# Thresholded attention on one core: the stages of a pair of heads placed by a plan of 22 steps

## The chip, the cores and the metric

One core of a Trainium2 chip runs the kernel once per launch. The metric is device time in microseconds, the median of three runs. TensorE (PE) is granted one of two clocks, 1.2 GHz or 2.4 GHz; the profile shows it as a share, 0.50 or 1.00. The other engines of this kernel are ScalarE (ACT), VectorE (DVE), GpSimd (POOL), whose queue here issues transfers, and SyncE (SP), which only issues transfers.

## The reference

Attention in f32 for 8 x 12 heads of 512 rows and 64 columns, with a cut: weights at or below 0.1 become zero, and what is left is normalised again.

```python
batch, heads, seq, dim = 8, 12, 512, 64          # threshold 0.1
scores = np.einsum('bhqd,bhkd->bhqk', Q, K) * scale
weights = softmax(scores)
weights = np.where(weights > threshold, weights, 0)
weights = weights / (np.sum(weights, axis=-1, keepdims=True) + 1e-10)
return np.einsum('bhqk,bhkd->bhqd', weights, V)
```

A row in which no weight exceeds 0.1 has an output of zero. With these inputs that is most rows.

## The kernel before

The kernel works on pairs of heads, 48 of them. The output is first filled with zeros, 256 KB per pair, from a tile of zeros (`do_load`, L174). Then a cheap screen in bf16 finds the rows that may have a weight above the threshold, at most 64 per head; these alone are gathered, computed exactly in f32, and scattered over the zeros.

A pair takes these stages, each a function of the code:

- **load** (SP): Q and K of the pair in four transfers, and the fill with zeros. **vload** (POOL): V, as bf16.
- **Q and K transposes** `do_tr` (PE, L180): four 128x128 f32 transposes each, into one PSUM bank; evicted by ACT (`do_qev` L186, `do_kev` L192). DVE centres K (`do_kcentre`).
- **scores** `do_qk` (PE, L227): in each of four steps two matmuls of 128x512, one per head, on the two halves of the array; **screen** `do_screen`: per step two score tiles, reduced by ACT (exponential with a sum, L241) or by DVE (maximum, L244). Of the eight tiles of a pair ACT takes five and DVE three.
- **squares, norms, normev**: a check of the norms that the screen's margin relies on (DVE, PE, ACT).
- **flags** (DVE, L248), **rank** (PE, L256 and L258), **key** (DVE, keys and the one-hot oh), **idx** (PE, L277), **gather** (DVE idx, L283, then POOL's indirect DMA, L284): from the flags of 512 rows the list of the selected ones, and their rows of Q.
- **split** (DVE, qb, L294), **xtr** (PE, L301), **xev** (ACT, xq, L307): the gathered rows, transposed.
- **xqk** (PE, L312): their exact scores, f32, in two passes of the profile's rows; **xexp** (ACT, e, L318), **xmask** (DVE, tv L324 and the mask m L326).
- **xpt** (PE, L334): four bf16 transposes of m; **xptev** (DVE, pt, L340); **xpv** (PE, L349 and L352): output and row sums; **xout**: the reciprocal rcp (DVE, L359 and L360), the scaled result res (ACT, L362) and the scatter (POOL, L363).

One loop of steps g runs over 4 steps a pair, hp being the pair whose scores the step makes, qi = 0 to 3. Each step issues the scores and stages of several pairs: of the next pair (its transposes), of this one, and of those one to four back. Every compute instruction and POOL's transfers keep the order in which the program gives them, per engine (`keep`); each engine takes its own list in order, and waits on semaphores for the others. The scheduler places the loads, with five buffers each for Q and K. The order by hand, before:

- qi 0: flags and rank of hp-1, Q transpose of hp+1, xqk of hp-3, screen, xptev of hp-4, squares of hp.
- qi 1: K transpose of hp+1, xpv of hp-4, screen, key of hp-1, the K eviction, xexp of hp-3.
- qi 2: idx of hp-1, screen, gather of hp-1, kcentre of hp+1, xmask of hp-3, split of hp-2, xout of hp-4.
- qi 3: xtr of hp-2, xpt of hp-3, norms of hp, vload, screen, xev of hp-2, normev of hp.

PSUM has eight banks: five for 128x512 f32 tiles (`spsum`: scores, transposes, xqk), one for the transposed mask (`ptpsum`), two small ones (`mpsum`, tag sm: norms, rank, idx, xtr, xpv). A stage that takes a bank waits until the last reader of its previous tile is done.

The fill with zeros and the scatter write the same DRAM tensor. The scheduler orders them against each other: a scatter waits until the fill ahead of it in its order has landed, and the next fill waits until that scatter has landed. This holds before and after the change.

At the end the kernel checks that no head had more than 64 selected rows and no norm was too large; otherwise a loop at the end computes everything without the screen. With these inputs it isn't entered.

Of the kernel before, what the change touches and what calls it, by code (L numbers as in the profile page):

```python
# [11 lines left out]
def kernel(  # L12
# [122 lines left out]
    nc.gpsimd.memset(cuts[:, 1, 0:SO - 1], CUT * CS / scale)  # L135
# [12 lines left out]
    ptpsum = ctx.enter_context(tc.tile_pool(name="ptpsum", bufs=1, space=bass.MemoryType.PSUM))  # L148
    mpsum = ctx.enter_context(tc.tile_pool(name="mpsum", bufs=2, space=bass.MemoryType.PSUM))
# [8 lines left out]
    qb_t, sq_t, nm_t = {}, {}, {}  # L158
# [25 lines left out]
    def do_qev(hp, sc):  # L184
        qk = tpool.tile([P, 2, SO * P], SCREEN)
        keep(nc.scalar.copy(qk[:, 0, :], sc[:]))  # L186
        qk_t[hp] = qk

    def do_kev(hp, sc):
# [17 lines left out]
    def do_norms(hp):  # L207
        nm = mpsum.tile([P, P], f32, name="sm")
# [22 lines left out]
    def do_screen(g):  # L231
# [5 lines left out]
        for h2 in range(2):  # L237
            sc = sc_t.pop((g, h2))
            if h2 == 0 or qi == SO - 1:
# [12 lines left out]
    def do_rank(hp):  # L252
        f = f_t[hp]
        rk = mpsum.tile([P, P], f32, name="sm")
# [18 lines left out]
    def do_idx(hp):  # L273
        oh = oh_t.pop(hp)[:].rearrange("p h s r -> p r (h s)")
        ix = mpsum.tile([P, P], f32, name="sm")
# [23 lines left out]
    def do_xtr(hp):  # L299
        xp = mpsum.tile([P, P], f32, name="sm")  # L300
# [29 lines left out]
    def do_xpt(hp):  # L330
        m = m_t.pop(hp)
        pt = ptpsum.tile([P, SO, P], bf16)
# [10 lines left out]
    def do_xpv(hp):  # L343
        pt, v_bf = pts_t.pop(hp), v_in.pop(hp)
        o = mpsum.tile([P, P], f32, name="sm")
# [10 lines left out]
    def do_xout(hp):  # L356
        o = o_t.pop(hp)
        rcp = small.tile([P, 1], f32)
        keep(nc.vector.tensor_scalar_add(rcp[:], o[:, D:D + 1], 1e-10))  # L359
        keep(nc.vector.reciprocal(rcp[:], rcp[:]))  # L360
        res = outp.tile([P, D], f32)
        keep(nc.scalar.activation(res[:], o[:, 0:D], ACTF.Copy, scale=rcp[:, 0:1]))  # L362
        keep(nc.gpsimd.indirect_dma_start(  # L363
            out=Or, out_offset=bass.IndirectOffsetOnAxis(ap=ix_t.pop(hp)[:, 0:1], axis=0),
            in_=res[:], in_offset=None, element_offset=hp * 2 * S * D, bounds_check=2 * S - 1, oob_is_err=False))
# [6 lines left out]
    do_qev(0, do_tr(q_in.pop(0)))  # L372
    do_kev(0, do_tr(k_in.pop(0)))
# [4 lines left out]
    def has(hp):  # L378
        return 0 <= hp < NP

    for g in range((NP + 5) * SO):
# [6 lines left out]
        if qi == 0:  # L388
            if has(hp - 1):
                do_flags(hp - 1)  # L390
                do_rank(hp - 1)
            if has(nxt):
                tr = do_tr(q_in.pop(nxt))
            if has(hp - 3):
                do_xqk(hp - 3)
            if g < G:
                do_screen(g)
            if has(nxt):
                do_qev(nxt, tr)
            if has(hp - 4):  # L400
                do_xptev(hp - 4)
            if has(hp):
                do_squares(hp)
        elif qi == 1:
            if has(nxt):
                tr = do_tr(k_in.pop(nxt))
            if has(hp - 4):
                do_xpv(hp - 4)
            if g < G:
                do_screen(g)  # L410
            if has(hp - 1):
                do_key(hp - 1)
            if has(nxt):
                do_kev(nxt, tr)
            if has(hp - 3):
                do_xexp(hp - 3)
        elif qi == 2:
            if has(hp - 1):
                do_idx(hp - 1)
            if g < G:  # L420
                do_screen(g)
            if has(hp - 1):
                do_gather(hp - 1)
            if has(nxt):
                do_kcentre(nxt)
            if has(hp - 3):
                do_xmask(hp - 3)
            if has(hp - 2):
                do_split(hp - 2)
            if has(hp - 4):  # L430
                do_xout(hp - 4)
        else:
            if has(hp - 2):
                do_xtr(hp - 2)
            if has(hp - 3):
                do_xpt(hp - 3)
            if has(hp):
                do_norms(hp)
            if has(hp + 2):
                do_vload(hp + 2)  # L440
            if g < G:
                do_screen(g)
            if has(hp - 2):
                do_xev(hp - 2)
            if has(hp):
                do_normev(hp)
# [10 lines left out]
    over_t = mpsum.tile([P, P], f32, name="sm")  # L457
# [9 lines left out]
    with tc.If(many > 0):  # L467
        with tc.For_i(0, NP, 1) as hp:
# [9 lines left out]
            for qi in range(SO):  # L478
                for h2 in range(2):
# [12 lines left out]
                    pt_ps = ptpsum.tile([P, SO, P], bf16, name="pt")  # L492
# [5 lines left out]
                    o = mpsum.tile([P, P], f32, name="sm")  # L498
# [47 lines left out]
```

## Time and profile before

| | us |
|---|---|
| median of 3 runs | 482.33 (480.74 to 484.32) |
| the profiled execution | 484.83 |
| its span, first to last instruction | 483.1 |
| PE busy (matmuls) | 355.0 |
| DVE busy | 259.6 |
| ACT busy | 261.3 |
| POOL busy | 140.3 |

The mean granted clock over the span is 0.684. A row of a timeline gives the start from the beginning of the span, the duration, engine, line, operation and tiles; a number in brackets is the idle time of the engine before it and what ended it. Matmuls overlap, so that what one costs PE is read from its start to the next one's start.

### The profile page before, as it was taken

Reading aid. Unit: us, or ns where it says so; the run is one execution under the profiler, and the core shown is the slowest. Engines: PE = TensorE matmul, PEld = TensorE weight load, DVE = VectorE, ACT = ScalarE, POOL = GpSimd, SP = SyncE. Lnnn points to the kernel's source line nnn. Section 1 sums busy time; section 2 is a strip of 40 time slices with the busy share of each in tenths; the row PEclk is TensorE's granted clock in tenths of the full one; section 3 lists DMA queues with packets and bytes.
Section 4 is the critical chain, followed back from the end, with each engine's and each line's share of the span. In section 5 each row is a group of like instructions: output and inputs, shape, how many; then the busy total and the mean of one; then the engine's idle time right before and its main releaser. Section 6 shows DMA issues by size and latency. Waiting matters only on the chain. (4 is left out here: it accounts for less than half of the span.)

```text
span 483.1 us, 7777 instructions
## 1 busy us (share of the span) xinstructions
PE 355.0 (73%) x2450; PEld 182.8 (38%) x2450; DVE 259.6 (54%) x729; ACT 261.3 (54%) x865; POOL 140.3 (29%) x172
## 2 busy tenths in 40 slices
PE   3878876887788678867886787688768867886861
PEld 2444333433434343434343433344343434343330
DVE  2565465556555654565456555555555565556540
ACT  3675465555645564556455556555565556564520
POOL 5122223223322332233223322432242233223221
PEclk9996667666766676677667666766676667666555
DMA  7994544454344435443544445445434441311000
GB/s 161 234 230 90 127 107 91 88 117 108 83 94 117 102 81 105 108 103 80 118 96 100 88 88 127 93 90 122 97 87 95 119 100 39 67 15 13 6 3 7
DMA packets 124461, 45.87 MB, mean 95 GB/s; under 512 B 104758, under 2 KB 118272, under 8 KB 124416
## 3 DMA queue, kind: packets, MB, share of 16 engines
q1 hardware_dynamic: 108288, 37.76, 30.3%
q0 software_dynamic: 16128, 7.57, 12.9%
q8 instruction: 21, 0.34, 0.3%
q14 instruction: 24, 0.20, 0.1%
HBM read 39.32 MB, written 14.16 MB: 111 GB/s over the span
## 5 line engine op out<-in xcount | busy, mean ns | idle before, releaser
L241 ACT ACTIVATE junk<-sc 128x512 bf16<-128x512 f32 x240 | 143.9, 603 | 77.5 <-PE sc L227 77.4
L244 DVE TENSOR_REDUCE stat<-sc 128x1 f32<-128x512 f32 x144 | 99.1, 688 | 123.0 <-PE sc L227 122.1
L284 POOL DMA_INDIRECT qsel<-in_Q_dram,idx x48 | 50.9, 1060 | 278.2 <-DVE idx L283 253.8
L227 PE MATMUL sc<-qk 64*128 64x512 bf16 x384 | 99.9, 515 | 2.0 <-DVE qk L197 1.8
L312 PE MATMUL sc<-kt,xq 128*128 128x512 f32 x96 | 91.6, 1058 | 0.0
L301 PE MATMUL sm<-identity_f,qb 128*128 128x128 f32 x48 | 18.4, 384 | 83.0 <-DVE qb L294 83.0
L363 POOL DMA_INDIRECT out_dram<-res,idx x48 | 48.9, 1019 | 54.7 <-ACT res L362 47.6
L362 ACT ACTIVATE res<-sm,rcp 128x64 f32<-128x64 f32 x48 | 15.1, 314 | 79.5 <-DVE rcp L360 72.9
L180 PE MATMUL sc<-identity_f,q_sb 128*128 128x128 f32 x192 | 49.4, 408 | 5.1 <-POOL heads L130 4.6
L241 ACT ACTIVATION_READ_ACCUMULATOR junk<-sc 128x1 f32 x240 | 50.6, 211 | 0.0
L180 PE MATMUL sc<-identity_f,k_sb 128*128 128x128 f32 x192 | 49.2, 406 | 2.0 <-DMA k_sb<-in_K_dram 1.9
L227 PEld LDWEIGHTS <-qk 64*128 64x128 bf16 x384 | 19.5, 98 | 73.4 <-issue 71.3
L186 ACT CAST qk<-sc 128x512 bf16<-128x512 f32 x48 | 28.1, 586 | 33.0 <-PE sc L180 33.0
L248 DVE TENSOR_TENSOR f<-stat,cuts 128x8 bf16<-128x8 f32 x48 | 8.0, 167 | 70.2 <-ACT junk L241 69.3
L301 PEld LDWEIGHTS sm<-identity_f,qb 128*128 128x128 f32 x48 | 7.3, 152 | 99.1 <-DVE qb L294 99.1
L180 PEld LDWEIGHTS sc<-identity_f,k_sb 128*128 128x128 f32 x192 | 31.7, 202 | 21.1 <-issue 21.1
L167 POOL DMA_DIRECT2D v_bf<-in_V_dram x48 | 37.4, 779 | 1.2 <-issue 1.2
L326 DVE SCALAR_TENSOR_TENSOR m<-e,tv 128x512 bf16<-128x512 f32 x48 | 36.1, 751 | 1.7
L192 ACT ACTIVATE kt<-sc 128x512 f32<-128x512 f32 x48 | 28.6, 596 | 13.9 <-PE sc L180 13.9
L180 PEld LDWEIGHTS sc<-identity_f,q_sb 128*128 128x128 f32 x192 | 32.0, 204 | 5.6 <-POOL heads L130 4.6
L204 DVE TENSOR_TENSOR sq<-qk 128x1024 bf16<-128x1024 bf16 x48 | 32.6, 679 | 0.0
L318 ACT ACTIVATE e<-sc 128x512 f32<-128x512 f32 x48 | 28.4, 593 | 6.6 <-PE sc L312 6.6
(64 smaller groups left out, 384.5 us busy)
## 6 DMA issues: line engine op xcount, KB each, us to landing
q_sb<-in_Q_dram SPq DMA_DIRECT2D x96, 128.0 KB, 3.2
k_sb<-in_K_dram SPq DMA_DIRECT2D x96, 128.0 KB, 2.9
out_dram<-zero SPq DMA_DIRECT2D x48, 256.0 KB, 3.1
v_bf<-in_V_dram POOLq DMA_DIRECT2D x48, 128.0 KB, 3.2
qsel<-in_Q_dram,idx POOLq DMA_INDIRECT x48, 2.5
out_dram<-res,idx POOLq DMA_INDIRECT x48, 2.2
```

Source lines behind the costliest of these rows:

```text
L167: keep(nc.gpsimd.dma_start(out=v_bf[:], in_=Vf[hp]))
L180: keep(nc.tensor.matmul(sc[:, r * P:(r + 1) * P], lhsT=src[:, r, :], rhs=identity_f32[:], is_transpose=True, start=True, stop=True))
L192: keep(nc.scalar.activation(kt[:], sc[:], ACTF.Copy, accum_out=ksum[:]))
L204: keep(nc.vector.tensor_tensor(out=sq[:], in0=qk[:], in1=qk[:], op=ALU.mult))
L227: keep(nc.tensor.matmul(sc[:], lhsT=qk_t[hp][ps, 0, qi * P:(qi + 1) * P], rhs=qk_t[hp][ps, 1, :], start=True, stop=True))
L241: keep(nc.scalar.activation(junk[:], sc[:], ACTF.Exp, scale=BETA * scale / CS, accum_out=stat[:, h2, qi:qi + 1]))
L244: keep(nc.vector.tensor_reduce(stat[:, h2, qi:qi + 1], sc[:], axis=AX.X, op=ALU.max))
L284: keep(nc.gpsimd.indirect_dma_start(out=qsel_bufs[hp % NS][:], out_offset=None, in_=Qr, in_offset=bass.IndirectOffsetOnAxis(ap=idx[:, 0:1] ...
L312: keep(nc.tensor.matmul(sc[:], lhsT=xq_t.pop(hp)[:], rhs=k_t.pop(hp)[:], start=True, stop=True))
L318: keep(nc.scalar.activation(e[:], xs_t.pop(hp)[:], ACTF.Exp, scale=scale, accum_out=sum1[:]))
L326: keep(nc.vector.scalar_tensor_tensor(out=m[:], in0=e[:], scalar=tv[:, 0:1], in1=e[:], op0=ALU.is_gt, op1=ALU.mult))
L363: keep(nc.gpsimd.indirect_dma_start(out=Or, out_offset=bass.IndirectOffsetOnAxis(ap=ix_t.pop(hp)[:, 0:1], axis=0), in_=res[:], in_offset=N ...
```

## The change

The hand-written order per qi is replaced by a table, `PLAN`, with for each of PE, ACT and DVE the step, counted from the first scores of a pair, at which a stage of this pair is issued. Step t of pair hp comes in step 4 hp + t of the loop. Within a step the loop issues the scores on PE, then PE's stages, then the screen, then DVE's stages, then ACT's; of several stages of one engine that fall in a step, the one with the larger t (the older pair) comes first.

```diff
+    PLAN = {
+        "pe": {-4: [do_ktr], -3: [do_qtr], 1: [do_norms], 5: [do_rank], 7: [do_idx], 12: [do_xtr],
+               14: [do_xqk], 18: [do_xpt], 20: [do_xpv]},
...
+    LAST = 22
+
+    def run(engine, g):
+        for t in sorted(PLAN[engine], reverse=True):
+            hp, at = divmod(g - t, SO)
+            if at == 0 and 0 <= hp < NP and (hp > 0 or t >= 0):
+                for step in PLAN[engine][t]:
+                    step(hp)
+
+    for g in range(G + LAST):
         hp, qi = divmod(g, SO)
-        nxt = hp + 1
-        if qi == 0 and has(hp + PRE):
+        if qi == 0 and PRE <= hp + PRE < NP:
             do_load(hp + PRE)
+        if qi == 3 and hp + 2 < NP:
+            do_vload(hp + 2)
         if g < G:
             do_qk(g)
...
+        run("pe", g)
+        if g < G:
+            do_screen(g)
+        run("dve", g)
+        run("act", g)
```

The other two engines' stages stand at these steps: ACT kev -4, qev -3, normev 2, xev 12, xexp 15, xout 21; DVE kcentre -2, squares 0, flags 4, key 6, gather 8, split 11, xmask 17, xptev 19, xrcp 21. K is now transposed ahead of Q.

The split of xout into two (`do_xrcp` on DVE, `do_xout` with ACT's part and the scatter), the PSUM pools and the screen:

```diff
-    ptpsum = ctx.enter_context(tc.tile_pool(name="ptpsum", bufs=1, space=bass.MemoryType.PSUM))
-    mpsum = ctx.enter_context(tc.tile_pool(name="mpsum", bufs=2, space=bass.MemoryType.PSUM))
+    mpsum = ctx.enter_context(tc.tile_pool(name="mpsum", bufs=3, space=bass.MemoryType.PSUM))
...
-            if h2 == 0 or qi == SO - 1:
+            if h2 == 0 or qi == 2:
                 junk = junkp.tile([P, SO * P], bf16)
...
-        pt = ptpsum.tile([P, SO, P], bf16)
+        sm = mpsum.tile([P, SO, P], bf16, name="smt", tag="sm")
+        pt = sm
...
-    def do_xout(hp):
-        o = o_t.pop(hp)
+    def do_xrcp(hp):
+        o = o_t[hp]
         rcp = small.tile([P, 1], f32)
         keep(nc.vector.tensor_scalar_add(rcp[:], o[:, D:D + 1], 1e-10))
         keep(nc.vector.reciprocal(rcp[:], rcp[:]))
+        rc_t[hp] = rcp
```

The one step in which ACT screens both heads is now the third of a pair and no longer the fourth; the constants that the flags compare with follow it. The transposed mask takes one of three small banks that norms, rank, idx, xtr and xpv use too.

Three places show what moves. First PE around xtr, the transpose of the gathered rows (qb); in a row stand line, operation, output and inputs with their buffer numbers, and the output's shape. Before:

```order
L227 LDWEIGHTS qk_3161
L227 MATMUL sc_3365<-qk_3161 128x512
L301 MATMUL sm_3367<-identity_f32_58,qb_3353 128x128
L334 LDWEIGHTS m_3351
L334 MATMUL pt_3369<-identity_bf_63,m_3351 128x128
```

And now, where L361 is the end of xpv, L309 xtr, L180 the K transpose and L235 the scores:

```order
L361 MATMUL sm_3492<-ones_bf_70,pt_3474 128x1
L309 MATMUL sm_3505<-identity_f32_58,qb_3476 128x128
L180 MATMUL sc_3507<-identity_f32_58,k_sb_3222 128x128 x4
L235 LDWEIGHTS qk_3438
L235 MATMUL sc_3530<-qk_3438 128x512
```

xtr stood behind the scores of the fourth step and ahead of the mask's transposes; it now stands behind xpv, with the K transpose and the scores of the second step following it.

Second, PE around xqk, the exact scores. Before (L258 is the end of rank, L180 here the Q transpose):

```order
L258 MATMUL sm_3405<-f_3403,ones_bf_70 128x2
L180 MATMUL sc_3410<-identity_f32_58,q_sb_3132 128x128 x4
L312 MATMUL sc_3415<-kt_2935,xq_3389 128x512
L227 LDWEIGHTS qk_3291
L227 MATMUL sc_3427<-qk_3291 128x512
```

And now, where L343 is the mask's transposes and L320 is xqk:

```order
L343 LDWEIGHTS m_3431
L343 MATMUL smt_3444<-identity_bf_63,m_3431 128x128
L320 MATMUL sc_3449<-kt_2877,xq_3395 128x512
L235 LDWEIGHTS qk_3308
L235 MATMUL sc_3462<-qk_3308 128x512
```

xqk moved from behind the rank and the Q transpose to behind the mask's transposes, which belong to an older pair; the scores of the fourth step follow it.

Third, DVE, from the maximum of the fourth step's (before) and second step's (now) scores on. Before:

```order
L244 TENSOR_REDUCE stat<-sc 128x1
L283 TENSOR_SCALAR idx<-sm,slot_base 128x1
L197 TENSOR_SCALAR qk<-kt,ksum 128x512
L324 TENSOR_SCALAR tv<-sum_3849 128x1
L326 SCALAR_TENSOR_TENSOR m<-e,tv 128x512
L294 TENSOR_TENSOR qb<-qsel_98,half 128x128
L359 TENSOR_SCALAR rcp<-sm 128x1
L360 RECIPROCAL rcp<-rcp 128x1
```

And now:

```order
L252 TENSOR_REDUCE stat<-sc 128x1
L368 TENSOR_SCALAR rcp<-sm 128x1
L369 RECIPROCAL rcp<-rcp 128x1
L332 TENSOR_SCALAR tv<-sum_3739 128x1
L334 SCALAR_TENSOR_TENSOR m<-e,tv 128x512
L273 TENSOR_TENSOR keys<-sm,f 128x8
L275 TENSOR_TENSOR oh<-slot_no,keys 128x512
L205 TENSOR_SCALAR qk<-kt,ksum 128x512
L252 TENSOR_REDUCE stat<-sc 128x1
L349 COPY pt<-smt 128x512
L302 TENSOR_TENSOR qb<-qsel_99,half 128x128
```

The split (qb) stood right behind the mask m; it now comes behind the eviction of the transposed mask (pt), six rows behind m, and the reciprocal stands ahead of the mask.

## Rows read from the trace of the kernel before

**Rows 1.** The page, part 1: busy time, share and instructions of each engine.

```profile
PE 355.0 (73%) x2450; PEld 182.8 (38%) x2450; DVE 259.6 (54%) x729; ACT 261.3 (54%) x865; POOL 140.3 (29%) x172
```

**Rows 2.** Waits: engine and line, released by: us in total, times, longest.

```profile
PE sm L301 <- DVE qb L294: 83.0, 48, 1.8
```

**Rows 3.** Timeline of PE, 248.5 to 252.6: start, duration, what.

```profile
248.56 1.91 PE L312 MATMUL sc<-kt,xq 128*128 128x512 f32 x2
250.40 0.61 PE L227 MATMUL sc<-qk 64*128 64x512 bf16 x2
250.94 1.11 PE L180 MATMUL sc<-identity_f,k_sb 128*128 128x128 f32 x4
251.99 0.44 PE L349 MATMUL sm<-v_bf,pt 128*64 128x64 bf16 x8
```

**Rows 4.** Timeline of PE, 260.2 to 266.0.

```profile
260.28 0.39 PE L227 MATMUL sc<-qk 64*128 64x512 bf16 x2
260.61 0.66 PE L180 MATMUL sc<-identity_f,k_sb 128*128 128x128 f32 x4
261.19 0.33 PE L349 MATMUL sm<-v_bf,pt 128*64 128x64 bf16 x8
...
261.64 0.39 PE L227 MATMUL sc<-qk 64*128 64x512 bf16 x2
...
264.41 0.33 PE L301 MATMUL sm<-identity_f,qb 128*128 128x128 f32 x1 [1.78 <-DVE qb L294]
264.58 0.39 PE L334 MATMUL pt<-identity_bf,m 128*128 128x128 bf16 x4
```

**Rows 5.** Timeline of DVE, 254.3 to 258.9.

```profile
254.36 0.15 DVE L324 TENSOR_SCALAR tv<-sum 128x1 f32<-128x1 f32 x1
254.54 0.75 DVE L326 SCALAR_TENSOR_TENSOR m<-e,tv 128x512 bf16<-128x512 f32 x1
...
255.60 0.17 DVE L360 RECIPROCAL rcp<-rcp 128x1 f32<-128x1 f32 x1
...
257.39 0.68 DVE L244 TENSOR_REDUCE stat<-sc 128x1 f32<-128x512 f32 x1
257.99 0.41 DVE L340 COPY pt<-pt 128x512 bf16<-128x512 bf16 x1
```

**Rows 6.** Timeline of DVE, 260.2 to 262.5.

```profile
260.74 0.69 DVE L244 TENSOR_REDUCE stat<-sc 128x1 f32<-128x512 f32 x1 [1.75 <-PE sc L227]
```

**Rows 7.** Stretches: length, busy (x) of PE, PEld, DVE, ACT, POOL, PEclk, DMA, GB/s.

```profile
256.60:260.10 3.50, 3.16 (x14) 1.43 (x12) 1.70 (x4) 2.08 (x8) 1.58 (x2) 0.50 0.34 40
260.10:263.00 2.90, 2.54 (x27) 1.30 (x26) 2.09 (x6) 2.23 (x8) 0.00 (x0) 1.00 0.74 202
263.00:266.90 3.90, 1.73 (x23) 1.28 (x24) 2.29 (x9) 2.43 (x11) 2.69 (x3) 1.00 0.27 61
447.70:451.30 3.60, 3.26 (x16) 0.87 (x13) 1.70 (x4) 1.59 (x8) 0.91 (x1) 0.50 0.03 8
451.30:456.50 5.20, 3.17 (x35) 1.84 (x33) 3.35 (x12) 3.54 (x13) 2.46 (x2) 0.50 0.01 4
```

**Rows 8.** Timeline at three places: scores of pair 4, last rank, last scatter.

```profile
36.30 0.61 PE L227 MATMUL sc<-qk 64*128 64x512 bf16 x2
...
456.54 0.19 PE L256 MATMUL sm<-f,tri 128*128 128x8 bf16 x1 [0.88 <-ACT norms L218]
...
474.46 0.98 POOL L363 DMA_INDIRECT out_dram<-res,idx  x1 [1.86 <-ACTq L467]
```

**Rows 9.** The page, part 6: issues, KB each, median us to landing.

```profile
out_dram<-zero SPq DMA_DIRECT2D x48, 256.0 KB, 3.1
...
qsel<-in_Q_dram,idx POOLq DMA_INDIRECT x48, 2.5
out_dram<-res,idx POOLq DMA_INDIRECT x48, 2.2
```

**Rows 10.** DMA issues of the stretch 15 to 42, same columns.

```profile
out_dram<-zero SPq DMA_DIRECT2D x5, 256.0 KB, 3.9
```

More of the change, by code (lines that the diff above doesn't have):

```diff
@@ L207, in do_norms @@
     def do_norms(hp):
-        nm = mpsum.tile([P, P], f32, name="sm")
+        nm = mpsum.tile([P, P], f32, name="sm", tag="sm")
         sq = sq_t.pop(hp)
@@ L253, in do_rank @@
         f = f_t[hp]
-        rk = mpsum.tile([P, P], f32, name="sm")
+        rk = mpsum.tile([P, P], f32, name="sm", tag="sm")
         cnt = rk[:, 0:2 * SO].rearrange("p (h r) -> p h r", h=2)
@@ L274, in do_idx @@
         oh = oh_t.pop(hp)[:].rearrange("p h s r -> p r (h s)")
-        ix = mpsum.tile([P, P], f32, name="sm")
+        ix = mpsum.tile([P, P], f32, name="sm", tag="sm")
         for r in range(SO):
@@ L299, in do_xtr @@
     def do_xtr(hp):
-        xp = mpsum.tile([P, P], f32, name="sm")
+        xp = mpsum.tile([P, P], f32, name="sm", tag="sm")
         keep(nc.tensor.matmul(xp[:], lhsT=qb_t.pop(hp)[:].rearrange("p h d -> p (h d)"), rhs=identity_f32[:],
@@ L344, in do_xpv @@
         pt, v_bf = pts_t.pop(hp), v_in.pop(hp)
-        o = mpsum.tile([P, P], f32, name="sm")
+        o = mpsum.tile([P, P], f32, name="sm", tag="sm")
         for h2 in range(2):
@@ L360, in do_xout @@
         keep(nc.vector.reciprocal(rcp[:], rcp[:]))
+        rc_t[hp] = rcp
+    def do_xout(hp):
         res = outp.tile([P, D], f32)
-        keep(nc.scalar.activation(res[:], o[:, 0:D], ACTF.Copy, scale=rcp[:, 0:1]))
+        keep(nc.scalar.activation(res[:], o_t.pop(hp)[:, 0:D], ACTF.Copy, scale=rc_t.pop(hp)[:, 0:1]))
         keep(nc.gpsimd.indirect_dma_start(
             out=Or, out_offset=bass.IndirectOffsetOnAxis(ap=ix_t.pop(hp)[:, 0:1], axis=0),
-            in_=res[:], in_offset=None, element_offset=hp * 2 * S * D, bounds_check=2 * S - 1, oob_is_err=False))
+            in_=res[:], in_offset=None, element_offset=hp * 2 * S * D,
+            bounds_check=2 * S - 1, oob_is_err=False))
     PRE = 3
@@ L371 @@
         do_vload(hp)
-    do_qev(0, do_tr(q_in.pop(0)))
-    do_kev(0, do_tr(k_in.pop(0)))
+    do_ktr(0)
+    do_kev(0)
+    do_qtr(0)
+    do_qev(0)
     do_kcentre(0)
     G = NP * SO
-    def has(hp):
-        return 0 <= hp < NP
-    for g in range((NP + 5) * SO):
+    PLAN = {
+        "pe": {-4: [do_ktr], -3: [do_qtr], 1: [do_norms], 5: [do_rank], 7: [do_idx], 12: [do_xtr],
+               14: [do_xqk], 18: [do_xpt], 20: [do_xpv]},
+        "act": {-4: [do_kev], -3: [do_qev], 2: [do_normev], 12: [do_xev], 15: [do_xexp], 21: [do_xout]},
+        "dve": {-2: [do_kcentre], 0: [do_squares], 4: [do_flags], 6: [do_key], 8: [do_gather],
+                11: [do_split], 17: [do_xmask], 19: [do_xptev], 21: [do_xrcp]},
+    }
@@ L456 @@
     nc.vector.tensor_reduce(over[:], most[:], axis=AX.X, op=ALU.max)
-    over_t = mpsum.tile([P, P], f32, name="sm")
+    over_t = mpsum.tile([P, P], f32, name="sm", tag="sm")
     nc.tensor.matmul(over_t[0:1, :], lhsT=over[:], rhs=identity_f32[:], start=True, stop=True)
@@ L497 @@
                     nc.scalar.copy(pt[:], pt_ps[:])
-                    o = mpsum.tile([P, P], f32, name="sm")
+                    o = mpsum.tile([P, P], f32, name="sm", tag="sm")
                     for kj in range(SO):
```

78 lines of the change are left out of this document (13 added, 65 removed).

## The prediction

> **What bounds the kernel now.** I read the page's busy shares first, then the waits, then TensorE's rows in one pair of heads at either clock, then stretches of time with the granted clock. No engine fills the span: PE 73%, ACT 54%, DVE 54% [rows 1]. Per pair (48 of them) PE is busy 355.0 / 48 = 7.4 us, DVE 5.4, ACT 5.4. The 44 pairs from the first scores of pair 4 (36.30) to the rank after the last scores (456.54) [rows 8] take 420.2 / 44 = 9.55 us each. So about 2 us a pair is time in which PE waits, and the largest part of it is one wait per pair, for the split of the gathered queries: 83.0 us in 48 times, 1.7 us each [rows 2].
>
> PE's own work has two sizes. At a granted clock of 0.50 (1.2 GHz) the exact scores (xqk, L312) take 1.84 us from their start to the next, the K transpose 1.05, two score matmuls 0.54 [rows 3]. At 1.00 (2.4 GHz) the K transpose takes 0.58, two score matmuls 0.32 to 0.33 [rows 4]. Which clock is granted goes with what PE did before: after 256.6 to 260.1, where PE was busy 3.16 of 3.50 us, it rose to 1.00, and in 260.1 to 263.0 (busy 2.54 of 2.90) it stayed there; after 263.0 to 266.9, where PE was busy only 1.73 of 3.90, the clock had fallen to 0.50 again by the next xqk (the mean of the stretch is still 1.00) [rows 7]. The wait thus costs twice: its own 1.8 us, and the slow clock behind it.
>
> **The change, part by part.** The instructions and their number stay the same; a pair still has 8 score matmuls, 8 f32 transposes, and so on. What moves is their place. All that PE needs is now issued on another engine one step earlier in the program, except where an engine lags. So the sum is made by following the slowest ring of hand-overs through a pair of the new order, at 2.4 GHz, with durations of before. Ring, from the end of the mask m on DVE:
>
> 1. PE starts after a hand-over of 0.07 (the score matmuls of 260.28 end at 260.67, the reduction starts at 260.74 [rows 4, 6]); the mask's transposes xpt take 0.39 [rows 4]. Then xqk, which no row shows wholly at 2.4 GHz: at least half of its 1.84, 0.92, and at most 1.84; by the ratios of the other two (0.32 / 0.54, 0.58 / 1.05) it is 1.02 to 1.09, by the half 0.92. I take 1.00. Sum 1.46.
> 2. The next scores go out; from their start to the start of DVE's reduction it is 0.46 (260.28 to 260.74). The reduction takes 0.60 until the next start, the eviction pt 0.41 [rows 5], hand-over 0.07. Sum 1.54.
> 3. PE, which waits in order for pt, runs xpv 0.45 (261.19 to 261.64), xtr 0.17 (264.41 to 264.58), the K transpose 0.58, the next scores; 0.46 to DVE's reduction. Sum 1.66.
> 4. DVE: reduction 0.60, two small operations for rcp of 0.17 each, tv 0.18, m 0.75 [rows 5]. Sum 1.87.
>
> The ring closes at 1.46 + 1.54 + 1.66 + 1.87 = 6.53 us a pair. PE has other work of the pair to do beside steps 2 and 4 (two pairs of scores and the small index matmuls beside 2; rank, norms, the Q transpose and two pairs of scores beside 4), so that by estimate it idles some 0.7 us before xpv and again before xpt; the wait of 1.8 us before xtr goes, since the split now comes on DVE right behind pt's eviction, and on PE xpv (0.45) stands between the wait for pt and xtr. What is late next is the mask, and after it pt. That ring is also why PE doesn't come free of the other engines: it runs ahead of DVE within a step, so "the preceding step" isn't over when PE asks.
>
> What the edits cost besides. The screen by exponential moved from step 3 to step 2 of a pair: ACT has as many as before, nothing added. PSUM: xpt takes a bank of the three small ones, which ACT's res has to have left; in the ring res comes some 0.6 us before the mask ends (it needs rcp, the mask needs rcp, tv and m), so it is hidden, and costs its lateness one for one if ACT falls behind. The gather: its index is now followed by the split after 3 steps and not 4, that is 0.75 x 6.53 = 4.9 us, against 2.5 from issue to landing [rows 9] and an estimated 0.5 for the index and POOL's start; hidden with 1.9 to spare, and beyond that a late landing holds DVE in order, with the next index queued behind it. Loads: K is now transposed before Q and a step earlier; that only matters at the start, where PE waits for data: there a transpose and a pair of score matmuls (1.05 + 0.54 = 1.6) come to stand behind K of pair 1. I bound this by 0 and 3 and take 1.6.
>
> Will the clock hold? What the rows show of its fall is a stretch in which PE paused for 1.78 us in one piece, at 264.41 [rows 4, 7]; in the 2.90 us ahead, with 0.36 of pauses, it held. The ring's pauses of 0.7 us lie between. The nearer row is the one that held, since the long pause is gone. I take 2.4 GHz except for two pairs at the start of the full pipeline.
>
> At 1.2 GHz the same ring takes 0.84 (xqk), 0.47 (K transpose) and twice 0.22 (scores) more, and an estimated 0.2 for xpt, xpv and xtr: 8.5 us.
>
> A rule that speaks against the change: the Trainium skill (TensorE: Matmul & The Clock Gate, Part 4: PE-mode transpose) says that transposes by matmul don't count as activity that lifts the clock. By it the f32 transposes that now fill PE's row would leave the clock low. The rows point the other way: 447.7 to 451.3 has PE busy 3.26 of 3.60 us with xqk but without transposes of Q or K (the last pair has no next one), and the clock stayed 0.50 in the 5.2 us behind it; 256.6 to 260.1 has no more busy time and the four transposes of Q, and the clock rose [rows 7]. By the rule the sum would be that of the ring at 1.2 GHz, which is a rival below.
>
> The sum, against the profiled execution (span 483.1, 484.83 with what lies around it):
> - start of pair 4: 36.3 + 1.6 = 37.9
> - 44 pairs x 6.53 = 287.3
> - two pairs at 1.2 GHz, 2 x 2.0 = 4
> - tail: last rank to last scatter, 474.46 - 456.54 = 17.9, a chain of one pair's stages, which the new order keeps
> - from there to the end of the span 483.1 - 474.46 = 8.6
>
> Together 355.7; with 1.7 around the span 357.4. The median of the three runs shown is 0.5% below the profiled one (482.33 against 484.83), which brings it to 356. That is 26% less time than before.
>
> **The rivals.**
>
> *The clock doesn't hold.* For it: the rows show no stretch at 1.00 with two pauses of 0.7 us in a pair, so its holding is not seen but inferred. It would give, with all pairs at 1.2 GHz, 37.9 + 44 x 8.5 + 17.9 + 8.6 - 0.3 = 438; with half of them, 397. Against it: at 0.50 the ring leaves PE almost no pause, as in 256.6 to 260.1, behind which the clock rose [rows 7], so the new order lifts its own clock again when it has fallen. Chance 0.20, mostly for a part of the pairs.
>
> *The writes to the output take over.* The scatter of a pair and the fill with zeros write the same tensor, so the scheduler lets each wait for the landing of the other, in turn: scatter 2.2 us, fill 3.1 us [rows 9], and an estimated 0.3 for the two starts, 5.6 us a round. At 9.55 a pair nobody sees it. At 6.5 it is just hidden; with the landing of the busy start, 3.9 for the fill [rows 10] and by the same ratio 2.8 for the scatter, the round is 7.0, and the kernel takes 37.9 + 44 x 7.0 + 26.5 = 372. The transfers per pair stay, the pairs come 1.5 times as often, so landings will lengthen somewhat. Chance 0.12, with 360 to 400.
>
> *The same round, slower than before.* Should both landings grow until the round passes 9.55, which takes 9.2 us for the two against 5.3 now, the scatter on POOL would hold the V load and the gather behind it, and all would follow it. At a round of 10 us: 37.9 + 440 + 26.5 = 504. Only a saturated memory queue could do that, and the rows at the busiest time show 3.9 for the fill. Chance 0.04.
>
> *PE really never waits.* Then DVE's own 5.4 us a pair is the bound: 37.9 + 44 x 5.4 + 26.5 = 302. The order speaks against it: xpt follows the mask of one step earlier in the same breath, and the ring has no free place. Chance 0.05.
>
> **How the numbers follow.** The forecast (ring at 2.4 GHz) has 0.57, with its own range 340 to 375: xqk at 0.92 instead of 1.00 is 44 x 0.08 = 3.5 us less and the start without its 1.6 as much again; a late ACT or some pairs at the lower clock are put at up to 0.4 us a pair more, 18 us. The clock rival has 0.20, the writes 0.12, PE never waiting 0.05, slower 0.04, and no change, in which the old waits come back under other names, 0.02. About 1% is what a measurement of this kernel can tell from no change. Faster by more than that: 0.57 + 0.20 + 0.12 + 0.05 = 0.94; the same 0.02; slower 0.04. The range of 338 to 410 takes in the forecast's own range, the writes and the clock held for half of the pairs; outside are PE never waiting, the clock low throughout (some 0.05 of the 0.20), and no gain: less than 2 in 10.
>
> **What would show it.** Right: one pair takes 6.5 us in the middle; the granted clock is 1.00 in most of it; PE's waits are for m before xpt and for pt before xpv, 0.7 us each, and the wait for the split before xtr is gone; xqk takes about 1.0. Wrong: a granted clock that still alternates with pairs of 7 to 8.5 us; POOL's scatter waiting for the fill, or SyncE's fill for the scatter, in every pair; a wait for res in front of xpt, or DVE waiting for the gather. A pair of more than 9.5 us would overturn all of it.

## The result, and the profile after

The median is 344.6 us (342.8 to 348.7, four runs), against 483.3 for the kernel before in the same session: a ratio of 0.712, 95% interval 0.707 to 0.718. One of the four, 348.7, ran over 1.5% longer than the fastest at a lower granted clock (0.887), and the ratios here leave such runs out. The forecast was 356, the range 338 to 410. The profiled execution took 345.39 us, its span 343.8.

The page of the kernel after, parts 1 (busy time, share of the span, instructions) and 2 (TensorE's granted clock in 40 slices of 8.6 us):

```profile
PE 261.3 (76%) x2450; PEld 137.5 (40%) x2450; DVE 258.3 (75%) x729; ACT 257.8 (75%) x865; POOL 153.7 (45%) x173
...
PEclk9999999998599999999999899989999999996555
```

DVE is busy as long as before [rows 1], PE 94 us less with the same matmuls: they run at the higher clock. Three engines are now at 75% each, so this kernel has no engine that fills its span either.

The waits (engine and line, released by: us in total, times, longest), the answer to [rows 2]:

```profile
PE smt L343 <- DVE m L334: 28.4, 46, 1.3
PE sm L358 <- DVE pt L349: 26.8, 45, 0.9
DVE idx L291 <- DMA out_dram<-res,idx: 2.8, 5, 1.1
```

The wait of 1.7 us a pair ahead of xtr is gone; PE waits for the mask and for pt, 0.6 us each. SyncE's own queue shows that the fills with zeros wait for a scatter's landing in 39 of the 48 pairs (first row); before, they did so 4 times (second row):

```profile
SPq L174 <- DMA out_dram<-res,idx: 103.6, 39, 6.9
...
SPq L174 <- DMA out_dram<-res,idx: 28.2, 4, 8.8
```

A whole undisturbed pair on PE, as [rows 3, 4] showed it before, from xpv (L358) of one pair to that of the next (the first row here is xpv, L309 xtr, L343 xpt, L320 xqk):

```profile
200.71 0.33 PE L358 MATMUL sm<-v_bf,pt 128*64 128x64 bf16 x8 [0.59 <-DVE pt L349]
...
201.08 0.31 PE L309 MATMUL sm<-identity_f,qb 128*128 128x128 f32 x1
201.23 0.60 PE L180 MATMUL sc<-identity_f,k_sb 128*128 128x128 f32 x4
201.76 0.39 PE L235 MATMUL sc<-qk 64*128 64x512 bf16 x2
...
204.07 0.40 PE L343 MATMUL smt<-identity_bf,m 128*128 128x128 bf16 x4 [0.58 <-DVE m L334]
204.30 1.08 PE L320 MATMUL sc<-kt,xq 128*128 128x512 f32 x2
205.31 0.39 PE L235 MATMUL sc<-qk 64*128 64x512 bf16 x2
...
206.84 0.33 PE L358 MATMUL sm<-v_bf,pt 128*64 128x64 bf16 x8 [0.60 <-DVE pt L349]
```

The pair takes 206.84 - 200.71 = 6.13 us. DVE in the same pair, as in [rows 5, 6], and at the end a row of the pair behind it:

```profile
201.57 0.68 DVE L212 TENSOR_TENSOR sq<-qk 128x1024 bf16<-128x1024 bf16 x1
202.22 0.69 DVE L252 TENSOR_REDUCE stat<-sc 128x1 f32<-128x512 f32 x1
...
203.26 0.75 DVE L334 SCALAR_TENSOR_TENSOR m<-e,tv 128x512 bf16<-128x512 f32 x1
...
205.77 0.69 DVE L252 TENSOR_REDUCE stat<-sc 128x1 f32<-128x512 f32 x1 [0.82 <-PE sc L235]
206.38 0.41 DVE L349 COPY pt<-smt 128x512 bf16<-128x512 bf16 x1
...
208.50 0.68 DVE L252 TENSOR_REDUCE stat<-sc 128x1 f32<-128x512 f32 x1
```

PE waits 0.59 for DVE's pt and DVE waits 0.82 for PE's scores, in one pair: neither is the bound, the ring between them is. At one place it is almost a tie. From pt to the reduction at 202.22 DVE works through its own list (qb, a reduction, idx, the flags, the squares) without a pause. That reduction comes 0.46 behind PE's scores (201.76), as one does that waits for them, but only 0.65 behind the squares (201.57). In the pair behind, where idx starts 0.17 later, the squares (207.90) take 0.60 to the reduction at 208.50, which comes 0.61 behind the scores (207.89): there DVE's own list decides, and the pair takes 6.28. So a faster xpv, xtr or K transpose on PE would by estimate shorten the pair by about 0.05 and no more.

The three places of [rows 8] after (scores of pair 4, last rank, last scatter):

```profile
35.83 0.39 PE L235 MATMUL sc<-qk 64*128 64x512 bf16 x2
...
316.61 0.21 PE L264 MATMUL sm<-f,tri 128*128 128x8 bf16 x1
...
335.01 0.98 POOL L375 DMA_INDIRECT out_dram<-res,idx  x1 [3.52 <-DVEq L444]
```

| term of the sum | forecast | measured |
|---|---|---|
| start of pair 4 | 37.9 | 35.8 |
| 44 pairs to the last rank | 287.3 + 4 | 316.6 - 35.8 = 280.8 |
| from there to the last scatter | 17.9 | 18.4 |
| to the end of the span | 8.6 | 8.8 |
| sum | 355.7 | 343.8 |

At 6.13 the 44 pairs would be 269.7; the other 11.1 us lie mostly in nine longer pairs at five places. The stretches of the worst of them and of a good one (length, busy of PE, PEld, DVE, ACT, POOL, granted clock, DMA share, GB/s):

```profile
83.50:91.60 8.10, 7.71 (x54) 3.59 (x52) 5.32 (x16) 5.45 (x19) 3.79 (x4) 0.51 0.61 129
...
198.20:204.30 6.10, 4.93 (x54) 2.67 (x52) 5.38 (x16) 5.28 (x19) 2.39 (x3) 1.00 0.69 148
```

So one pair at 1.2 GHz takes 8.2 us (xqk at 83.45, the next at 91.64), and at 2.4 GHz 6.13. That is 1.4 less than the 9.55 a pair before, which ran at clocks between the two; so the order by itself is worth at least some 1.4 a pair by this one cold pair. How the other 2.1 divide between order and clock it doesn't tell.

### The profile page after: what moved, and what is told of

It is laid out like the page before. It is cut to its first block, busy times and chain, and to the rows that moved or that the text cites. A ratio compares the mean times of both kernels' runs of the same rounds, so it can differ in the third digit from the quotient of the medians.

```text
span 343.8 us, 7868 instructions
## 1 busy us (share of the span) xinstructions
PE 261.3 (76%) x2450; PEld 137.5 (40%) x2450; DVE 258.3 (75%) x729; ACT 257.8 (75%) x865; POOL 153.7 (45%) x173
## 5 line engine op out<-in xcount | busy, mean ns | idle before, releaser
L292 POOL DMA_INDIRECT qsel<-in_Q_dram,idx x48 | 62.1, 1293 | 121.5 <-DVE f L256 103.1
L235 PE MATMUL sc<-qk 64*128 64x512 bf16 x384 | 80.2, 414 | 0.7 <-ACT qk L194 0.7
L320 PE MATMUL sc<-kt,xq 128*128 128x512 f32 x96 | 59.9, 709 | 0.0
L343 PE MATMUL smt<-identity_bf,m 128*128 128x128 bf16 x192 | 20.5, 234 | 28.4 <-DVE m L334 28.4
L200 ACT ACTIVATE kt<-sc 128x512 f32<-128x512 f32 x48 | 28.7, 598 | 17.6 <-PE sc L180 17.6
L235 PEld LDWEIGHTS <-qk 64*128 64x128 bf16 x384 | 18.4, 94 | 58.5 <-issue 56.0
L180 PE MATMUL sc<-identity_f,k_sb 128*128 128x128 f32 x192 | 31.8, 292 | 10.0 <-DMA k_sb<-in_K_dram 10.0
L358 PE MATMUL sm<-v_bf,pt 128*64 128x64 bf16 x384 | 16.3, 207 | 26.8 <-DVE pt L349 26.8
L180 PE MATMUL sc<-identity_f,q_sb 128*128 128x128 f32 x192 | 33.6, 302 | 0.0
L205 DVE TENSOR_SCALAR qk<-kt,ksum 128x512 bf16<-128x512 f32 x48 | 27.0, 563 | 6.9 <-ACT kt L200 6.9
L180 PEld LDWEIGHTS sc<-identity_f,k_sb 128*128 128x128 f32 x192 | 24.2, 151 | 12.2 <-POOL cuts L136 6.6
L343 PEld LDWEIGHTS <-m 128*128 128x128 bf16 x192 | 11.7, 102 | 42.5 <-DVE m L334 42.5
L358 PEld LDWEIGHTS <-pt 128*64 128x64 bf16 x384 | 10.8, 115 | 43.1 <-DVE pt L349 40.1
```

The lines of the kernel that those rows point to most:

```text
L180: keep(nc.tensor.matmul(sc[:, r * P:(r + 1) * P], lhsT=src[:, r, :], rhs=identity_f32[:], is_transpose=True, start=True, stop=True))
L235: keep(nc.tensor.matmul(sc[:], lhsT=qk_t[hp][ps, 0, qi * P:(qi + 1) * P], rhs=qk_t[hp][ps, 1, :], start=True, stop=True))
L292: keep(nc.gpsimd.indirect_dma_start(out=qsel_bufs[hp % NS][:], out_offset=None, in_=Qr, in_offset=bass.IndirectOffsetOnAxis(ap=idx[:, 0:1] ...
L320: keep(nc.tensor.matmul(sc[:], lhsT=xq_t.pop(hp)[:], rhs=k_t.pop(hp)[:], start=True, stop=True))
L343: keep(nc.tensor.matmul(pt[:, kj, :], lhsT=m[:, kj * P:(kj + 1) * P], rhs=identity_bf[:], is_transpose=True, start=True, stop=True))
```

## The experiments

### Is it the ring?

One more maximum over 128x512 on DVE in each pair, at two places. In the ring, ahead of the mask:

```diff
+        pad = small.tile([P, 1], f32)
+        keep(nc.vector.tensor_reduce(pad[:], zero[:], axis=AX.X, op=ALU.max))
         tv = small.tile([P, 1], f32)
```

> One more maximum over 128x512 f32 (about 0.6 us) on DVE for each pair, right ahead of tv and the mask m. Theory A (ring): it stands in the ring, so the pair grows by its whole length: 6.13 to 6.7 to 6.8, some 371 to 376. Rival B (throughput of DVE, 5.4 busy of 6.13, with 0.7 free): nothing or up to 0.1 a pair, 344 to 350.

Measured 365.8 us, in one run. One xqk and the next:

```profile
147.40 1.08 PE L320 MATMUL sc<-kt,xq 128*128 128x512 f32 x2
...
154.13 1.08 PE L320 MATMUL sc<-kt,xq 128*128 128x512 f32 x2
```

The pair is 6.73 instead of 6.13: 0.60 more, the whole of the added operation (152.32 to 152.91 to the next start, in its timeline on DVE). Three pairs of the 48 were disturbed by over 1 us, so that the total came out below the 371 expected. PE's pause ahead of xpt is twice as long here, 1.17 beside the 0.60 ahead of xpv, and the granted clock stays up all the same, at 0.98 from 53 to 300 (columns as above):

```profile
153.90 0.40 PE L345 MATMUL smt<-identity_bf,m 128*128 128x128 bf16 x4 [1.17 <-ACT qk L194]
...
53.00:300.00 247.00, 183.76 (x1845) 98.43 (x1844) 214.51 (x577) 195.59 (x650) 113.66 (x108) 0.98 0.64 139
```

The same two lines behind `do_kcentre`, where DVE waited 0.82 us:

> The same added maximum, but right behind kcentre, where DVE then waits some 0.8 us for the scores of the next step. Theory A (ring): it takes the place of that wait, 0 to 0.1 a pair, 344 to 350. Rival B (DVE's throughput sets the pair): the same growth as ahead of the mask, 0.6 a pair, 371 to 376.

Measured 342.4 us, in one run, and the pairs:

```profile
190.38 0.65 PE L322 MATMUL sc<-kt,xq 128*128 128x512 f32 x1
...
196.51 1.08 PE L322 MATMUL sc<-kt,xq 128*128 128x512 f32 x2
```

6.13 again, with DVE busy 285.2 us instead of 258.3. The same work on the same engine costs all or nothing by its place. The ring is shown; DVE's throughput is not the bound. No operation was added on PE, so its steps of the ring are read from the rows alone.

### What the PSUM part is worth

```diff
-    mpsum = ctx.enter_context(tc.tile_pool(name="mpsum", bufs=3, space=bass.MemoryType.PSUM))
+    ptpsum = ctx.enter_context(tc.tile_pool(name="ptpsum", bufs=1, space=bass.MemoryType.PSUM))
+    mpsum = ctx.enter_context(tc.tile_pool(name="mpsum", bufs=2, space=bass.MemoryType.PSUM))
```

> Undoes the PSUM part alone: two small banks and one for the transposed mask, as before, with the plan of the kernel after. Theory A (ring): with two small banks in turn the norms and the rank have to wait for the bank that xpv's output holds until ACT's res, in the step in which PE is late already: 0.4 to 0.9 a pair more, 362 to 386. Rival B (three banks instead of two and one are not needed, since the wait for pt has PE idle anyway): the same, 342 to 348.

Measured 447.4 us, ratio to before 0.922 (0.915 to 0.930): of the 138 us that the change brought, 103 are lost by this edit. The number of small banks is the same, three; what differs is whether the transposed mask has one of its own or shares all three with the others. Theory A had the wait and not its size. The wait and the stretch of 53 to 398 us, with its granted clock:

```profile
PE sm L222 <- ACT res L374: 53.0, 43, 1.2
...
53.00:398.00 345.00, 261.32 (x2015) 129.85 (x2015) 215.63 (x593) 219.71 (x709) 126.24 (x120) 0.76 0.48 104
```

The norms wait 1.24 us for the bank that xpv's output holds until ACT's res. With the waits for pt (0.4 to 0.6) and for xtr's bank (0.42, read as the wait for DVE's idx, which reads that bank) PE pauses some 2.0 to 2.3 us in a pair, where it is 1.2 in the kernel after and 1.8 in the run with the maximum ahead of the mask. The clock, 0.97 in the kernel after from 53 to 300 and 0.98 in that run, falls to 0.76: pairs of 9.2 and 7.9 us mostly alternate. In the longer of the two, whose xqk start at 206.50 and 215.71, the norms:

```profile
213.53 0.35 PE L222 MATMUL sm<-heads,sq 128*128 128x2 bf16 x8 [1.24 <-ACT res L374]
```

The plan without the sharing of the three banks gives 35 us, with it 138. What the sharing would give the old order wasn't run, and no run separates the longer waits from the lower clock in the 103.

### What the moved screen is worth

```diff
-            if h2 == 0 or qi == 2:
+            if h2 == 0 or qi == SO - 1:
```

(and the constants of the flags with it).

> Undoes the screen part alone: ACT reduces both heads' scores in the fourth step of a pair, as before, and DVE in the first, second and third. Theory A (ring): no reduction then stands on DVE ahead of pt (it comes in the fourth step), and one more is in the third, so the ring loses about 0.6 and its hand-over; the pair falls to 5.5 to 5.9, or to the 6.1 of the round of output writes: 320 to 345. Rival B (ACT with two screens right before res and xexp of that step is late, and the bank that its res has to leave is late with it, as in the run with two small banks): pairs of 6.4 to 8, 355 to 420.

Measured 349.3 us, ratio to before 0.725 (0.720 to 0.731), by the ratios some 1.8% more than the kernel after. Undisturbed pairs are shorter, 5.72 us, as the ring says:

```profile
99.48 1.08 PE L319 MATMUL sc<-kt,xq 128*128 128x512 f32 x2
...
103.60 0.34 PE L220 MATMUL sm<-heads,sq 128*128 128x2 bf16 x8 [0.63 <-ACT xq L314]
...
105.20 1.08 PE L319 MATMUL sc<-kt,xq 128*128 128x512 f32 x2
```

In the second row the norms wait, by the name in the brackets for the bank that ACT's xq has to leave, which is rival B's mechanism at another stage. And most pairs aren't undisturbed: DVE's idx waits for a scatter's landing 16.8 us in 25 times, and pairs take from 5.7 to 7.9. Neither theory alone had this right. The move of the screen made the pair longer and steadier; a shorter ring met something else, which the next runs are about.

### The long pairs, and what lies behind the ring

`do_gather` writes idx into a pool of four buffers. Its pair's scatter reads it 13 steps later, so idx, four pairs on, waits for that scatter's landing: the row of DVE's idx above. In the kernel after, POOL at the time of one such wait:

```profile
218.88 1.02 POOL L375 DMA_INDIRECT out_dram<-res,idx  x1 [3.30 <-DMA out_dram<-zero]
```

The scatter waited 3.30 us for a fill that had been issued at 213.45, DVE's idx then 1.06 for a scatter's landing (at 221.06), and the pair in which this falls and the one behind it took 7.4 and 7.3. So six buffers for idx:

```diff
+    idxp = ctx.enter_context(tc.tile_pool(name="idx", bufs=6))
-        idx = small.tile([P, 1], i32)
+        idx = idxp.tile([P, 1], i32)
```

> The row numbers of selected rows (idx) get a pool of their own with six buffers; in the kernel after they come from a pool of four, so DVE's idx waits for the landing of the scatter four pairs back. In the trace after DVE waits there 5 times, 2.8 us in total (longest 1.06), and each wait stands ahead of a long pair: some pairs take 6.5 to 8.2 us and not 6.13, together about 10 us. Theory A (these waits trip the long pairs and the falls of the clock): the waits are gone, nearly all pairs take 6.13, time 334 to 339 against 345. Rival B (long pairs come from elsewhere, such as late landings for the loads, or clock falls of their own): same time, 342 to 348, with long pairs left.

Measured 341.3 us, ratio 0.707 (0.701 to 0.713), which the interval of the kernel after overlaps: unclear, and nearer to rival B. The waits for idx went, and others came:

```profile
POOL out_dram L376 <- DMA out_dram<-zero: 21.0, 7, 3.2
...
DVE qb L303 <- DMA qsel<-in_Q_dram,idx: 5.2, 7, 3.0
```

The buffers were only where a late round of the output writes showed first. Behind a waiting scatter POOL's queue holds the V load and the next gather; so now DVE waits for the gathered rows.

Next, the fill left out (the line `nc.sync.dma_start(out=Oz[hp], in_=zero[:])`):

> Leaves out the fill of the output with zeros (48 transfers of 256 KB): rows that are not selected are not written. The rest is as in the kernel after. Theory A (the ring of hand-overs between PE and DVE sets the pair at 6.13 us): the undisturbed pairs keep 6.13; what goes are the long pairs, as scatters land at once: 333 to 337. Rival B (the writes to the output, fill and scatter in turn, 2.7 + 2.2 + issue of about 0.3 each, set the pair): the pair falls below 6.0 and the time below 330.

Measured 333.2 us, ratio 0.688 (0.682 to 0.693). The pairs keep 6.13, in all but two or three of the 48, here from the xqk at 98.91 to the next:

```profile
105.04 1.08 PE L319 MATMUL sc<-kt,xq 128*128 128x512 f32 x2
```

Theory A: at 6.13 the round of writes doesn't set the pair, it only disturbs it. The 11 us by which the median is lower aren't all disturbed pairs: in the two profiled executions, whose spans lie 7.5 apart, the scores of pair 4 start 2.2 earlier without the fill (33.64) and the 44 pairs behind take 5.0 less. With the fill its 12.6 MB of traffic went too, so that the order of the writes and the load on the transfers aren't told apart.

### Opening the ring

In each step DVE's stages now come ahead of DVE's own reduction of the step's scores (`do_screen` split into ACT's part and DVE's):

```diff
         if g < G:
-            do_screen(g)
+            do_screen(g, "act")
         run("dve", g)
+        if g < G:
+            do_screen(g, "dve")
         run("act", g)
```

> In each step DVE's stages (pt, m, rcp and the others) are issued ahead of DVE's own reduction of the step's scores; in the kernel after they come behind it. Nothing else is moved. Theory A (the ring m, xpt, xqk, scores, reduction, pt, xpv, xtr, K transpose, scores, reduction, rcp, tv, m sets the pair): two reductions and the way to them from the scores leave the ring (0.46 + 0.61 twice), PE no longer waits for pt and m, and the next bound decides: DVE's own 5.4 us or the round of the output writes, 5.6: a pair of 5.4 to 5.7, 310 to 328. Rival B (PE's throughput or the transfers already set 6.13): 340 to 348.

Measured 335.7 us, ratio 0.691 (0.683 to 0.699): faster than the kernel after, but far from 310 to 328. At the start it does what was expected: from the first xqk at 29.68 to the second it is 5.75 us, to the third another 5.24:

```profile
35.43 1.08 PE L323 MATMUL sc<-kt,xq 128*128 128x512 f32 x2
...
40.67 0.65 PE L323 MATMUL sc<-kt,xq 128*128 128x512 f32 x1
```

Then, from the fourth xqk at 46.6 to the forty-fourth at 298.8, they average 6.3, hardly less than the 6.4 of the kernel after; most of the 9 us gained lie at the start. PE's wait for pt is gone but for one of 0.5, as expected; its wait for m is not (21.3 us in 36 times against 28.4 in 46), which theory A had wrong. The wait that has come:

```profile
DVE idx L294 <- DMA out_dram<-res,idx: 24.6, 23, 2.4
```

With six buffers for idx as well:

> Both edits: DVE's stages ahead of its reduction, and six buffers for idx. If the waits for idx buffers trip the long pairs (theory A of the idx run), this is 5 to 15 us below the run with DVE's stages first alone, 300 to 318; at faster pairs, scatters are later in pairs, so the buffers matter more. If idx buffers don't matter: the same as that run.

Measured 361.7 us, ratio 0.753 (0.746 to 0.759): 26 us slower than without the buffers. Both expectations are wrong. Its waits:

```profile
DVE qb L306 <- DMA qsel<-in_Q_dram,idx: 65.5, 41, 2.9
...
POOL out_dram L379 <- DMA out_dram<-zero: 38.4, 11, 4.5
PE sm L313 <- DVE qb L306: 37.2, 29, 2.5
```

And POOL with DVE's split of the same time:

```profile
161.33 1.37 POOL L379 DMA_INDIRECT out_dram<-res,idx  x1 [3.90 <-ACT xq L319]
...
167.72 0.29 DVE L306 TENSOR_TENSOR qb<-qsel,half 128x128 f32<-128x128 f32 x1 [2.35 <-DMA qsel<-in_Q_dram,idx]
```

The first six pairs take 5.2 to 5.7. Then the scatter waits on POOL, 155 us in all 48 times by the rows of its line together, against 76 without the buffers (most of them name an engine that had long been done, as the first row above does); the V load and the gather (here at 163.77) stand behind it, the split waits for the gather, PE for the split, and the mean clock is 0.871 against 0.906 without the buffers. So the four idx buffers look like a throttle, which stopped DVE before POOL's queue ran into the fill: the cost of 26 us is measured, this reading of it comes from the waits. With the throttle away, the wait that the change had removed came back, now with the gather behind it.

With DVE's stages first and no fill (its output lacks the unselected rows):

> DVE's stages ahead of its reduction, and the fill with zeros left out, so that unselected rows of the output are not written. With DVE first alone the pairs took 5.2 to 5.7 at the start and then about 6.15 on average, with DVE's idx waiting 24.6 us in all for landings of scatters; with the fill left out alone they kept 6.13. Theory A (the ring through the reductions sets 6.13 in the kernel after; with DVE first the round of fill and scatter takes over): with both, the pair falls to 5.2 to 5.5 throughout, 295 to 308. Rival B (DVE first gains nothing of its own; about 6.1 is set by something common to all, such as ACT or PE): pairs of 6.0 to 6.2, 328 to 336.

Measured 311.7 us, ratio 0.644 (0.640 to 0.649): near theory A and outside its numbers. The undisturbed pairs take 5.24, here from the xqk at 261.34 to the next:

```profile
266.58 0.65 PE L322 MATMUL sc<-kt,xq 128*128 128x512 f32 x1
```

Most others take 5.5 to 6.1, since idx still waits for landings of scatters (12.3 us, 19 times), whether a fill is there or not: this wait is for the scatter alone.

Then two versions meant to be faster. Both have DVE's stages first, more buffers for idx, the fills of two pairs issued together (a scatter waits for a fill only every second time), and the stages from the split on later, four steps in the first and eight in the second (PE's line of the plan for the second; ACT's and DVE's move likewise):

```diff
-               14: [do_xqk], 18: [do_xpt], 20: [do_xpv]},
+               22: [do_xqk], 26: [do_xpt], 28: [do_xpv]},
...
-        nc.sync.dma_start(out=Oz[hp], in_=zero[:])
+        for z in range(hp, min(hp + 2, NP) if hp % 2 else 1):
+            nc.sync.dma_start(out=Oz[z], in_=zero[:])
```

> A version meant to be faster: DVE's stages ahead of its reduction, eight buffers for idx, the stages from the split on four steps later (so that the gather has seven steps and not three; six buffers for K transposed, four for the gathered rows), and the fills of two pairs issued together, so that a scatter waits for a fill only every second time. Theory A (with the ring gone the rest is lost to the round of fill and scatter, by way of idx, of the gather behind a waiting scatter, and of the clock): pairs of 5.2 to 5.7, 295 to 318. Rival B (bursts of two fills hold up the loads of Q and K or the scatters by more than they save): 330 to 365.

Measured 323.3 us (318.8 to 324.5): between the two theories. DVE still waits for the gather, 20.2 us in 20 times, so another four steps:

> As the deep version with the fills of two pairs together, with the stages from the split on another four steps later (buffers: seven for K transposed, ten for V, five for the gathered rows, ten for idx). In the deep version DVE waited 20.2 us in 20 times for a gather that stood on POOL behind a scatter that waited for two fills. Theory A (these late gathers are what is left above 5.24 a pair, with the falls of the clock that they bring): with eleven steps for the gather the wait goes, pairs of 5.24 to 5.5, the pipeline is four steps (about 4 us) longer at its end: 298 to 314. Rival B (the round of fill and scatter itself bounds, and comes out at another wait): 318 to 330.

Measured 315.6 us, ratio 0.652 (0.644 to 0.660): the fastest kernel here that computes everything, 8.5% below the kernel after, and 1.6 us above theory A's range. The wait for the gather fell, and a new one of the same kind came, for the three buffers of res:

```profile
ACT res L379 <- DMA out_dram<-res,idx: 9.7, 7, 2.3
...
DVE qb L307 <- DMA qsel<-in_Q_dram,idx: 6.6, 9, 1.7
```

Its undisturbed stretch of 60 to 120 us (columns as above) shows what bounds it there:

```profile
60.00:120.00 60.00, 56.10 (x592) 31.29 (x591) 58.85 (x173) 58.37 (x209) 29.70 (x30) 1.00 0.82 175
```

Pairs of 5.24, with DVE busy 98%, ACT 97% and PE 94%: engines, at last, and DVE the nearest to full, while PE still waits 0.31 for m in a pair. What is lost after that stretch (pairs up to 7.7) is by the waits the writes again; that part stays open. The two versions join several edits, and no run takes them apart.

### What lifts the clock

TensorE alone, in phases with pauses between them, in one run:

> Leaves out the whole attention: TensorE alone runs four phases with pauses of over 15 us in which DVE works: 280 f32 transposes by matmul, 560 bf16 transposes by matmul, 200 bf16 matmuls of 128x512, 280 f32 transposes again; a last small tile is all that is written. Theory A (f32 transposes lift the clock as matmuls do): the granted clock goes to 1.00 within each f32 phase. Rival B (the Trainium skill, page TensorE: Matmul & The Clock Gate, Part 4: PE-mode transpose: transposes don't count): it stays at 0.50 in the three phases of transposes and rises only in that of the matmuls. For the bf16 transposes neither case is read from the trace so far.

Stretches at the beginning and in the rest of phases two (bf16 transposes) and four (f32 transposes); columns are length, busy of PE, PEld, DVE, POOL, granted clock, DMA share, GB/s:

```profile
62.00:66.00 4.00, 4.00 (x40) 4.00 (x39) 0.00 (x0) 0.00 (x0) 0.50 0.00 0
66.00:95.00 29.00, 29.00 (x522) 29.00 (x519) 0.00 (x0) 0.00 (x0) 1.00 0.01 2
...
181.40:185.50 4.10, 4.10 (x20) 4.10 (x21) 0.00 (x0) 0.00 (x0) 0.51 0.00 0
185.50:214.00 28.50, 28.50 (x263) 28.44 (x261) 0.00 (x0) 0.00 (x0) 1.00 0.00 1
```

Both begin at 0.50 or 0.51 and go to 1.00, as the matmuls of phase three do (0.50 from 115.0 to 118.5, 0.98 behind it). Phase one (f32 transposes) shows no rise, since its record has 1.00 from the start. Theory A. The Trainium skill (TensorE: Matmul & The Clock Gate, Part 4: PE-mode transpose) says that transposes don't count; this run shows otherwise, for f32 and for bf16.

## Why the prediction was right

It was right: 344.6 lies in the range, and in the forecast's own range of 340 to 375, 3% below the forecast. Step by step, at the rows of 200 to 207:

- *The ring.* Shown by the two added operations (0.60 or 0.00 a pair). Its four steps: (1) 1.30 and not 1.46: the hand-over 0.06, xqk 1.01 as worked out, but xpt 0.23 (204.07 to 204.30), where 0.39 was taken, a row's duration and not the way from its start to the next start. That row had no clean reading: the norms behind it start 0.44 later (265.02). At 1.2 GHz the trace of before has the way, 0.42 (rows below), and by estimate half of it, 0.21, would have been near. (2) 1.53 (205.31 to 206.84), forecast 1.54. (3) xpv, xtr and the K transpose 1.05 (200.71 to 201.76) and 0.46 to the reduction, 1.51 for 1.66: xpv 0.37 for 0.45, xtr 0.15 for 0.17, the K transpose 0.53 for 0.58, all of which had been read from start to start, beside other neighbours. That DVE's own list from pt to the reduction is as long but for 0.05 wasn't worked out. (4) 1.79 (202.22 to the mask's end at 204.01) for 1.87, most of it the second operation for rcp, taken by its duration again: 0.17 for 0.08 from start to start. Sum 6.13 for 6.53, and 44 x 0.40 are the 17.6 us by which the ring's share was put too high; 7 of them came back in disturbed pairs, which is luck.

```profile
255.82 0.63 PE L334 MATMUL pt<-identity_bf,m 128*128 128x128 bf16 x4
256.24 0.40 PE L213 MATMUL sm<-heads,sq 128*128 128x2 bf16 x8
```

- *The waits.* 0.6 before xpt and 0.6 before xpv, forecast 0.7; none before xtr. PE doesn't come free of the other engines, as the text said; that the reductions stood in the ring was the reason, and with DVE's stages ahead of them the wait before xpv goes and the one before xpt shrinks to 0.3.
- *The clock.* It held through two pauses of 0.6 in a pair, which was inferred and not seen before. A cold pair takes 8.2, forecast 8.5. The 4 us for two of them at the start of the full pipeline were right neither in place (the clock is 1.00 from 33 to 53) nor in size: 11.1 us went into disturbed pairs further on. The rival of a clock that stays low has the low mean of the run with two small banks on its side (0.76), where waits of 1.24 and 0.42 more stand in a pair. Against it stands the run with the maximum ahead of the mask: 0.60 more in one of the two pauses, and the clock at 0.98. The 397 for half of the pairs cold is 395 by the sum's own terms, and nothing hangs on it.
- *PSUM.* That xpt's bank costs nothing held. That with two small banks the norms would wait in such a place, and that this one edit carries 103 us, the text didn't see.
- *The writes.* Priced at a round of 5.6 against 6.5. At 6.13 it still hid but for a few pairs. The fill's landings, which were to lengthen somewhat from 3.1, have a median of 2.7 in the six of 48 that the trace records; single ones were late, as the one issued at 213.45 that let the scatter go at 218.88. SyncE's fill waited for a scatter in 39 of 48 pairs, which the text had named as a sign of being wrong: it came, and the pair stayed at 6.13, so it was no such sign. The mechanism was right, and in the runs with a shorter ring most pairs beyond the undisturbed ones have waits of this kind (without the fill, for the scatter alone); that it shows in three places in turn (idx's buffers, the gather behind the scatter, res's buffers) was not in the text, which had only the queue on POOL.
- *PE never waiting*, DVE as the bound at 5.4 a pair: not this order, but 5.24 in the best version's stretch of 60 to 120, with PE's 0.31 for m left.
- *Start and tail.* 35.8 for 37.9, so that the 1.6 for K first was not paid; tail and end within 0.5 and 0.2.

What was only argued: that the clock falls in the kernel after came from the late rounds of writes. The order in time fits (a scatter's wait, idx's wait, long pairs, clock at 0.50), and without the fill one such place is left where five or so were (7.2 and 8.2 us, at 117 to 133), but no run separates a fall of the clock from the wait ahead of it.

## What to carry to other kernels

Where two engines each wait for the other in every round, add up the ring of hand-overs with pitches from start to start; a dummy operation put once inside and once outside shows whether the ring is there. A wait that is removed can be a throttle: before adding buffers, look which queue the faster engine will fill next, above all an in-order queue on which a waiting store stands ahead of a load that others need. And how small PSUM tiles share their banks can decide both TensorE's pauses and its clock: here three shared banks in place of two and one of its own were worth 103 of 138 us.

## What the runs showed of the hardware

- TensorE's granted clock rises from 0.50 to 1.00 in a phase of nothing but transposes, f32 or bf16, as in one of matmuls.
- A pair with nothing but short pauses can lose the high clock, but doesn't always: two of 0.6 us in a pair of 6.13 leave it at 0.97 on average from 53 to 300, pauses of 1.17 and 0.60 in a pair of 6.73 at 0.98; with three of about 1.24, 0.42 and 0.4 to 0.6 it is 0.76, and pairs mostly alternate between 9.2 and 7.9 us. What tells these cases apart the runs don't show.
- The f32 scores of 128x512 in two passes take 1.01 us from their start to the next at 2.4 GHz, half of 1.84 and a tenth more.
- A fill issued at 213.45, with loads of K and Q ahead of and behind it in SyncE's queue, let its scatter go only at 218.88, after a wait of 3.3 us; the median of the recorded landings is 2.7.
